# Where the low halves of the trunk weights are made: VectorE subtraction, or ScalarE negation and an accumulating DMA

## The chip, the core and the metric

The kernel runs on one core of a Trainium2 chip. The metric is device time in microseconds (us), median of the runs shown. All times are of the device alone: the host only lays the arrays out and puts the outputs together.

## What is computed

The reference is one inference step of a hybrid layer for 1,056 tokens of width 1,024 (1,024 of a prompt, 32 of a decoding request that shares the weights). Cut to what matters:

```python
z = rms_norm(x, g_mix) @ w_in                     # q, k, v, conv h/B/C, two gates
a = window_attention(q, k, v) @ w_attn_out
bo = (cb * causal_conv3(cc * ch)) @ w_conv_out
x = x + (sigmoid(ga) * a + sigmoid(gb) * bo) @ w_mix_out
cq = rms_norm(x, g_cross) @ w_cq                  # 1024 x 256
x = x + softmax(cq @ mem_k / 8) @ mem_v @ w_co    # 256 x 1024
x = x + square(relu(rms_norm(x, g_mlp) @ w_up)) @ w_down
y = rms_norm(x, g_final)
```

All of it is in fp32. The four matrices that the change speaks of are `w_conv_out` and `w_mix_out` (1,024 x 1,024 each), `w_cq` and `w_co`.

## The kernel before

**Products in two halves.** A product is made of three matmuls in the fp32r type. Each operand is split into a high part (the value rounded to fp32r) and a low part (what is left): `hi*hi + hi*lo + lo*hi`. `gemm` (L195 to L202) issues the three per 128 rows of the contraction: line L200 takes the weight's high half `wh` with the activation's high half, L201 `wh` with the low half of the activation, L202 the weight's low half `wl`. A weight tile is 128 x 1,024 (512 KB) and serves 24 matmuls of one chunk of tokens. The tokens are cut into three chunks of 384, 384 and 288 columns.

**The weights' way in.** `worder` lists the weights in the order of their use. `fetch_w` (from L145) loads the next one from HBM into a raw tile by SyncE's queue (L159). There are two raw tiles `wr`; from a certain item on (`third`, item 12 of the first chunk's trunk) every third weight goes to a third tile of another pool. `issue_w` (L164) makes `wh` by a ScalarE copy and `wl` by a VectorE subtraction, raw minus high (`split`, L128: L129 is the copy, L130 the subtraction). `wh` and `wl` have three buffers each. `next_w` runs this so that two or three weights stand ready ahead of the matmuls (`LOOK = 2`).

**Kept low halves.** The trunk is run once per chunk of tokens, so its weights come three times. For 8 of the 20 tiles (`kept`: the odd ones of `w_mix`, `w_cq` and `w_co`, and tiles 1 and 7 of `w_conv_out`), `wl` is written to a tile `wl_d` in HBM after it has been made (L179) and is loaded from there at the next uses (L172), so that VectorE isn't needed for it again; the raw tile is then needed for ScalarE's copy alone. For `w_cq` and `w_co` this ends before the third chunk.

**The stretch around the change.** The trunk lies between 797 and about 1,128 us of the profiled execution. Chunk 0: eight tiles of `w_conv_out`, the first of chunk 1, then eight of `w_mix`; no other product runs on TensorE beside them. Chunk 1: seven tiles of `w_conv_out`, eight of `w_mix`, with the cross attention of chunk 0 between them. Chunk 2: the same with 288 columns, with the cross attention of chunk 1 and the first tiles of `w_up` (the MLP) between them; at the end `w_co` of chunk 2. In the trunk, VectorE multiplies each result by a gate (L1068), and GpSimd adds the attention's part, which SyncE loads from `m_d` (L1064); that add (L1069) is where the operand of the next matrix comes from. For `w_mix`, GpSimd adds up squares for the norm (L276, L272).

**What sets the order.** The kernel is recorded with a scheduler that works on a modelled timeline and decides in which order each engine gets its instructions, within what the tiles' dependencies allow; instructions in `pin(...)` keep the order of the program. On the chip each engine, and each engine's DMA queue, then works strictly in that order: an instruction that waits holds up all that stand behind it on its engine.

Of the kernel before, what the change touches and what calls it, by code (L numbers as in the profile page):

```python
# [10 lines left out]
F32 = mybir.dt.float32  # L11
F32R = mybir.dt.float32r
AF = mybir.ActivationFunctionType
ALU = mybir.AluOpType
# [26 lines left out]
def hybrid_step(ctx: ExitStack, tc: tile.TileContext, io):  # L41
    nc = tc.nc
    act, dve, pool_e, pe, sp = nc.scalar, nc.vector, nc.gpsimd, nc.tensor, nc.sync
# [3 lines left out]
    def nm(s):  # L47
        uid[0] += 1
        return f"{s}_{uid[0]}"
# [78 lines left out]
    def split(hi, lo, src):  # L128
        act.copy(hi, src)  # L129
        dve.tensor_sub(lo, src, hi.bitcast(F32))  # L130

    def weight(key):
# [8 lines left out]
            src = src[j]  # L141
        return src

    fetched = []
    third = {}  # L145

    def fetch_w(raw=None):
        if raw is not None:
            pass
        elif third:  # L150
            third["n"] += 1
        if raw is not None:
            pass
        elif third and third["n"] % 3 == 0:
            raw = third["pool"].tile([P, 4, 256], F32, tag="ws", name=nm("wr3")).rearrange("p q c -> p (q c)")
        else:
            raw = wp.tile([P, 1024], F32, tag="wr", bufs=2, name=nm("wr"))
        src = weight(worder[wpos[0] + len(fetched)])
        load = sp.dma_start(raw.rearrange("p (i c) -> p i c", i=4) if len(src.shape) == 3 else raw, src)  # L159
        if third and third["n"] == 3 and third["pool"] is W["pool"]:  # L160
            pin(load)
        fetched.append(raw)

    def issue_w(pieces=(slice(0, 1024),)):  # L164
        if not fetched:
            fetch_w()
        raw = fetched.pop(0)
        key = worder[wpos[0]]
        hi = wp.tile([P, 1024], F32R, tag="wh", name=nm("wh"))
        lo = wp.tile([P, 1024], F32R, tag="wl", name=nm("wl"))  # L170
        if kept.get(key) is not None:
            sp.dma_start(lo.bitcast(F32), kept[key])  # L172
            act.copy(hi, raw)
        else:
            for at in pieces:
                split(hi[:, at], lo[:, at], raw[:, at])
            if key in kept:
                kept[key] = dram.tile([P, 1024], F32, name=nm("wl_d"))
                sp.dma_start(kept[key], lo.bitcast(F32))  # L179
        ready.append((worder[wpos[0]], (hi, lo)))  # L180
        wpos[0] += 1

    def next_w(key):
        while len(ready) <= LOOK and wpos[0] < len(worder) and worder[wpos[0]] is not STOP:
            issue_w()
        k, w = ready.pop(0)
        assert k == key, (k, key)
        return w
# [106 lines left out]
    def norm_x():  # L295
# [45 lines left out]
        with tc.manual_schedule(engines={mybir.EngineType.Activation, mybir.EngineType.DVE}):  # L341
            parts(0, range(1))
            issue_w((slice(0, 256), slice(256, 1024)))
            parts(0, range(1, NF))
            act.copy(ones_r, ones.to_broadcast([P, P]))
            issue_w()
            issue_w()
            squares(0)
# [115 lines left out]
    def do_K(pr, extras=()):  # L464
        def fn(w):
            kt = at_tile([P, NT], F32, "kt")
            ktt[pr] = kt
            for c, (o, n) in enumerate(CH):
                a = acc_tile([P, n])
                gemm(a, w, xg[c])  # L470
                dve.tensor_mul(kt[:, o : o + n], a, R[c])
                after(extras, c)
            sp.dma_start(io["o_k"][pr], kt[:, 896:])

        return fn
# [22 lines left out]
    def do_Q(kv, j, extras=()):  # L498
        def fn(w):
            for c, (o, n) in enumerate(CH):  # L500
                npr = min(n, NPR - o)
                if j == 0:
                    qs[kv, c] = at_tile([P, 4, npr], F32R, "QA" if c < 2 else "QB", 2 if c < 2 else 1)
                    if n > npr:
                        qs[kv, 3] = at_tile([P, 4, n - npr], F32R, "QC")
                a = acc_tile([P, n])
                gemm(a, w, xg[c])
                t = tmp(n)
                dve.scalar_tensor_tensor(t, a, 0.125, R[c], op0=ALU.mult, op1=ALU.mult)
                parts = [(qs[kv, c], slice(0, npr))]  # L510
                if n > npr:
                    parts.append((qs[kv, 3], slice(npr, n)))
                for q, s in parts:
                    for e in range(2):
                        own, other = slice(64 * e, 64 * e + 64), slice(64 - 64 * e, 128 - 64 * e)
                        h = 2 * j + e
                        act.copy(q[own, h], t[own, s])
                        dve.tensor_sub(q[other, h], t[own, s], q[own, h].bitcast(F32))
                after(extras, c)

        return fn
# [156 lines left out]
    def do_gate(to, extras=()):  # L678
        def fn(w):
            for c, (o, n) in enumerate(CH):  # L680
                a = acc_tile([P, n])
                gemm(a, w, xg[c])
                t = gate_slot(c, 0)
                dve.tensor_mul(t, a, R[c])
                act.activation(t, t, AF.Sigmoid)
                to(c, t)
                after(extras, c)

        return fn
# [18 lines left out]
    pieces = [("g", f, q) for f in PAIRS for q in range(2)]  # L708
# [42 lines left out]
    for i, h in enumerate(hosts):  # L751
# [16 lines left out]
        if h[0] == "Q":  # L768
            fn, key = do_Q(h[1], h[2], extras), qt(h[1], h[2])
        elif h[0] == "K":  # L770
            fn, key = do_K(h[1], extras), ("w_in", 8 + h[1])
        elif h[0] == "G":
            fn, key = do_gate(lambda c, t: sa.__setitem__((c, 0), t), extras), ("w_in", 34)
        else:
            fn, key = do_conv(*h, extras), conv_w(h[1], h[0])
# [932 lines left out]
    at = {}  # L1708
# [314 lines left out]
```

## Time and profile before

| | |
|---|---|
| median of 2 runs | 1754.41 us (1752.73 to 1756.1) |
| span of the profiled execution | 1747.8 us |
| TensorE busy (matmul) | 1727.7 us, 99% |
| VectorE busy | 1188.1 us, 68% |
| ScalarE busy | 852.9 us, 49% |
| GpSimd busy | 586.2 us, 34% |
| low halves made on VectorE (L130, `wl`, all weights) | 214 x 1,285 ns |
| DMA bytes moved | 346.60 MB |

The profile shows one execution. For that execution the profiler gives the span, from the first to the last instruction; the time of a run, measured without the profiler, is 4.9 to 8.3 us more than this span, 6.6 us at the median. In the rows, "busy" is the time in which an engine executes; an idle time is given with what ended it. SPq and POOLq are the queues from which SyncE and GpSimd issue DMAs. A line number is that of the kernel before.

### The profile page before, as it was taken

The numbers are of one execution on the slowest core, as the hardware profiler recorded it, in microseconds if no ns is written. First come the engines' busy times: TensorE is split into PE (matmuls) and PEld (weight loads), VectorE is DVE, ScalarE is ACT, GpSimd is POOL, SyncE is SP. The second block draws the span as 40 slices with busy tenths as digits, with TensorE's granted clock in tenths as the row PEclk, the third lists the DMA queues.
The fourth block names the chain that finished last, engine by engine and source line by source line (L and its number), as shares of the span: only waits on it lengthen the run. The fifth ranks groups of instructions, "written<-read, shape, count | busy, mean of one in ns | idle before, by whom it ended". The sixth has DMA issues, their size and how long they took to land. (4 is left out here: it accounts for less than half of the span.)

```text
span 1747.8 us, 32606 instructions
## 1 busy us (share of the span) xinstructions
PE 1727.7 (99%) x12262; PEld 1712.4 (98%) x12262; DVE 1188.1 (68%) x2276; ACT 852.9 (49%) x1660; POOL 586.2 (34%) x667
## 2 busy tenths in 40 slices
PE   9999999999999999999999999999999999999998
PEld 8999999999999999999999999999999999999998
DVE  7776777768666646555677888787666686545675
ACT  8653534535335324434556666765444463332444
POOL 0026366443553544432224232005555410000121
PEclk9999999999999999999999999999999999999999
DMA  4333344333436888867766667775666695555554
GB/s 185 104 126 128 114 134 153 115 139 127 160 132 204 296 292 280 291 203 238 264 213 198 221 227 241 235 258 191 217 222 219 219 330 185 188 193 169 192 170 160
DMA packets 179854, 346.60 MB, mean 198 GB/s; under 512 B 18657, under 2 KB 101249, under 8 KB 179569
## 3 DMA queue, kind: packets, MB, share of 16 engines
q1 hardware_dynamic: 163504, 290.07, 50.0%
q0 software_dynamic: 15568, 53.68, 8.8%
q8 instruction: 96, 1.57, 0.4%
q10 hardware_dynamic: 624, 0.77, 0.1%
q14 instruction: 62, 0.50, 0.1%
HBM read 250.73 MB, written 93.14 MB: 197 GB/s over the span
## 5 line engine op out<-in xcount | busy, mean ns | idle before, releaser
L129 ACT CAST wh<-wr 128x1024 fp32r<-128x1024 f32 (+1 forms) x214 | 223.8, 1046 | 366.6 <-PE acc L1810 121.4
L130 DVE TENSOR_TENSOR wl<-wr,wh 128x1024 fp32r<-128x1024 f32 (+1 forms) x214 | 275.0, 1285 | 106.2 <-ACT wh L129 105.4
L200 PE MATMUL acc<-X,wh 128*128 128x384 f32 (+1 forms) x864 | 281.5, 326 | 0.0
L201 PE MATMUL acc<-X,wh 128*128 128x384 f32 (+1 forms) x864 | 278.8, 323 | 0.1
L202 PE MATMUL acc<-X,wl 128*128 128x384 f32 (+1 forms) x864 | 277.8, 322 | 0.0
L276 POOL TENSOR_TENSOR xacc<-xacc,ct 128x384 f32<-128x384 f32 (+1 forms) x56 | 75.6, 1354 | 379.9 <-ACT ct L274 378.1
L201 PEld LDWEIGHTS acc<-X,wh 128*128 128x128 f32 x864 | 162.7, 188 | 1.7 <-DVE X L280 0.7
L200 PEld LDWEIGHTS acc<-X,wh 128*128 128x128 f32 x864 | 162.4, 188 | 0.8
L202 PEld LDWEIGHTS acc<-X,wl 128*128 128x128 f32 x864 | 162.4, 188 | 0.1
L200 PE MATMUL acc<-Y,wh 128*128 128x384 f32 (+1 forms) x432 | 139.9, 326 | 3.2 <-DVE ct L1068 2.9
L202 PE MATMUL acc<-Y,wl 128*128 128x384 f32 (+1 forms) x432 | 140.0, 325 | 2.7 <-DMA wl<-wl_d 2.7
L201 PE MATMUL acc<-Y,wh 128*128 128x384 f32 (+1 forms) x432 | 139.7, 324 | 0.0
L129 ACT CAST PTh<-pt 128x512 fp32r<-128x512 f32 (+3 forms) x94 | 45.8, 516 | 112.8 <-PE pt L598 111.4
L1809 PE MATMUL acc<-n,wh 128*128 128x264 f32 x352 | 100.2, 285 | 0.0
L1810 PE MATMUL acc<-n,wh 128*128 128x264 f32 x352 | 100.1, 284 | 0.0
L1811 PE MATMUL acc<-n,wl 128*128 128x264 f32 x352 | 99.9, 284 | 0.0
L735 POOL TENSOR_TENSOR ws<-ws 128x256 f32<-128x256 f32 x100 | 89.5, 895 | 5.6
L735 POOL TENSOR_TENSOR xacc<-xacc 128x256 f32<-128x256 f32 x100 | 86.8, 868 | 5.7 <-DMA xacc<-in_w_in 0.4
L200 PEld LDWEIGHTS acc<-Y,wh 128*128 128x128 f32 x432 | 81.4, 189 | 4.4 <-DVE ct L1068 3.8
L202 PEld LDWEIGHTS acc<-Y,wl 128*128 128x128 f32 x432 | 81.5, 189 | 3.0 <-DMA wl<-wl_d 3.0
L201 PEld LDWEIGHTS acc<-Y,wh 128*128 128x128 f32 x432 | 81.6, 189 | 0.0
L584 ACT ACTIVATE S<-S,nmx 128x257 f32<-128x257 f32 (+1 forms) x132 | 64.2, 488 | 18.9 <-DVE nmx L579 17.6
(432 smaller groups left out, 5554.9 us busy)
## 6 DMA issues: line engine op xcount, KB each, us to landing
wr<-in_w_up SPq DMA_DIRECT2D x53, 512.0 KB, 4.5
wr<-in_w_in SPq DMA_DIRECT2D x52, 512.0 KB, 3.6
wr<-wsum_d SPq DMA_DIRECT2D x40, 512.0 KB, 3.5
wr<-in_w_conv_out SPq DMA_DIRECT2D x24, 512.0 KB, 3.9
wr<-in_w_mix SPq DMA_DIRECT2D x24, 512.0 KB, 5.2
wr<-in_w_down SPq DMA_DIRECT2D x24, 512.0 KB, 3.6
n_d<-Z SPq DMA_DIRECT2D x32, 264.0 KB, 4.2
xacc<-in_w_down POOLq DMA_DIRECT2D x16, 512.0 KB, 4.5
```

The costliest lines, as they stand in the source:

```text
L129: act.copy(hi, src)
L130: dve.tensor_sub(lo, src, hi.bitcast(F32))
L200: pe.matmul(out, wh[:, a], hi, start=(k == 0), stop=False)
L201: pe.matmul(out, wh[:, a], lo, start=False, stop=False)
L202: pe.matmul(out, wl[:, a], hi, start=False, stop=(k == len(acts) - 1))
L276: pool_e.tensor_tensor(acc, acc, sq, op=ALU.add)
L584: act.activation(stl[:, h, : nk + 1], stl[:, h, : nk + 1], AF.Exp, scale=-1.0, bias=nmx[:, h : h + 1], accum_out=den[:, h : h + 1],)
L735: pin(pool_e.tensor_tensor(t[:, to], t[:, x], t[:, y], op=ALU.add))
L1809: pe.matmul(a, wh[:, s], hi, start=(t == 0 and k == 0), stop=False, skip_group_check=True)
L1810: pe.matmul(a, wh[:, s], lo, start=False, stop=False, skip_group_check=True)
L1811: pe.matmul(a, wl[:, s], hi, start=False, stop=(t == 1 and k == 7), skip_group_check=True)
```

## The change

```diff
+    BY_DMA = ("w_conv_out", "w_mix", "w_cq", "w_co")
...
         else:
-            for at in pieces:
-                split(hi[:, at], lo[:, at], raw[:, at])
+            if key[0] in BY_DMA:
+                act.copy(hi, raw)
+                act.mul(lo, hi.bitcast(F32), -1.0)
+                pool_e.dma_start(lo, raw, accum_op=ALU.add)
+            else:
+                for at in pieces:
+                    split(hi[:, at], lo[:, at], raw[:, at])
             if key in kept:
                 kept[key] = dram.tile([P, 1024], F32, name=nm("wl_d"))
                 sp.dma_start(kept[key], lo.bitcast(F32))
```

For a weight of the four matrices whose low half isn't loaded from `wl_d`, ScalarE makes the high half as before, and then writes its negative into `wl`. A DMA from GpSimd's queue then adds the raw weight to what stands in `wl`: minus high plus raw. VectorE has no part in it. The low halves of all other weights (`w_in`, `w_up`, `w_down`, the sums) are made as before. There are 46 such weights: 20 of `w_conv_out`, 16 of `w_mix`, 5 of `w_cq`, 5 of `w_co`. In the program, VectorE's instructions go from 2,061 rows to 2,015, ScalarE's from 1,321 to 1,367, GpSimd's from 509 to 555.

Behind the whole diff the line numbers grow by six (L1069 of before is L1075 after, L276 is L282, L810 is L816), between its two parts by one (L159 is L160), and those of `split` stay. After the change, L177 is ScalarE's copy, L178 the negation, L179 the accumulating DMA.

On GpSimd, at the beginning of chunk 0's trunk, before: the additions `ct` (L1069) of one `w_conv_out` tile after the other.

```order
L735 TENSOR_TENSOR ws_7775<-ws_7775 128x256 x4
L739 DMA usum_d<-ws_7775 128x2x256 x2
L1069 TENSOR_TENSOR ct_9363<-ct_9363,ct_9336 128x384
L1069 TENSOR_TENSOR ct_9415<-ct_9415,ct_9388 128x384
L1069 TENSOR_TENSOR ct_9467<-ct_9467,ct_9440 128x384
L1069 TENSOR_TENSOR ct_9519<-ct_9519,ct_9492 128x384
```

The same place after; `wl` is a low half, `wr` a raw tile, and the numbers are those of the buffers' use.

```order
L179 DMA wl_9256<-wr_9191 128x1024
L179 DMA wl_9278<-wr_9260 128x1024
L1075 TENSOR_TENSOR ct_9366<-ct_9366,ct_9339 128x384
L179 DMA wl_9335<-wr_9284 128x1024
L1075 TENSOR_TENSOR ct_9419<-ct_9419,ct_9392 128x384
L179 DMA wl_9388<-wr_9385 128x1024
L1075 TENSOR_TENSOR ct_9472<-ct_9472,ct_9445 128x384
L179 DMA wl_9441<-wr_9438 128x1024
```

Each addition is now followed by a DMA; the DMA of weight number n stands behind the addition that belongs to weight n-2.

On GpSimd at the change from chunk 0's `w_mix` to chunk 1's `w_conv_out`, after. Before, the additions L1069 of chunk 1's tiles stood behind each other here.

```order
L179 DMA wl_10147<-wr_10144 128x1024
L282 TENSOR_TENSOR xacc_9327<-xacc_9327,ct_10184 128x384
L1075 TENSOR_TENSOR ct_10226<-ct_10226,ct_10199 128x384
L1075 TENSOR_TENSOR ct_10267<-ct_10267,ct_10240 128x384
L179 DMA wl_10195<-wr_10192 128x1024
L179 DMA wl_10236<-wr_1800_10233 128x1024
```

Here two additions stand ahead of one DMA: the one of the weight next in use (`wl_10195`, tile 3 of `w_conv_out`) is behind the addition that belongs to tile 2.

On ScalarE in chunk 0's trunk, before and then after: the copy of the same two weights.

```order
L129 CAST wh_9436<-wr_9434 128x1024
L129 CAST M_9418<-ct_9415 128x384
L810 CAST Y_1600_9422<-ct_9378 128x384
L810 CAST Y_1602_9426<-ct_9380 128x384
L129 CAST wh_9488<-wr_9486 128x1024
```

```order
L177 CAST wh_9440<-wr_9438 128x1024
L178 ACTIVATE wl_9441<-wh_9440 128x1024
L129 CAST M_9475<-ct_9472 128x384
L816 CAST Y_1614_9479<-ct_9434 128x384
L816 CAST Y_1616_9483<-ct_9436 128x384
L177 CAST wh_9493<-wr_9491 128x1024
L178 ACTIVATE wl_9494<-wh_9493 128x1024
```

The negation L178 follows the copy at once; nothing stands between the two.

## The prediction

> **What bounds the kernel now.** I read the page first, then the waits of TensorE, then busy time by stretch, then the timeline of one raw weight buffer. The page's first lines:
>
> ```profile
> span 1747.8 us, 32606 instructions
> PE 1727.7 (99%) x12262; PEld 1712.4 (98%) x12262; DVE 1188.1 (68%) x2276; ACT 852.9 (49%) x1660; POOL 586.2 (34%) x667
> ```
>
> TensorE is the bound: 1727.7 of 1747.8 us, so 20 us is all that could be won by ending waits. VectorE, which the change relieves, is at 68%. Now the trunk alone, in four stretches: chunk 0 (two raw buffers), the `w_conv_out` part of chunk 1, its `w_mix` part, and chunk 2 (columns: from:to, length, busy time of PE, PEld, DVE, ACT and POOL, granted clock, DMA share, GB/s).
>
> ```profile
> 797.00:868.00 71.00, 71.00 (x409) 70.97 (x409) 44.54 (x68) 34.05 (x58) 17.96 (x12) 1.00 0.81 264
> 868.00:909.00 41.00, 38.32 (x219) 38.01 (x218) 29.80 (x49) 24.43 (x43) 12.37 (x9) 0.96 0.64 223
> 909.00:958.00 49.00, 49.00 (x295) 48.86 (x293) 37.67 (x60) 28.91 (x59) 20.20 (x17) 1.00 0.60 195
> 958.00:1128.00 170.00, 165.73 (x1249) 163.05 (x1248) 135.96 (x270) 114.98 (x246) 41.07 (x46) 1.00 0.68 225
> ```
>
> TensorE idles for 0 + 2.7 + 0 + 4.3 = 7 us in all of it. This bounds the gain: an empty VectorE could give back 7 us, 0.4%. The question is what the new way does to the lead with which weights are ready. The longest single wait of TensorE here is already one for a low half that comes by DMA:
>
> ```profile
> PE acc L202 <- DMA wl<-wl_d: 2.7, 1, 2.7
> ```
>
> The lead is set by the raw buffers. This is one turn of one of the two, in chunk 0, put together from the timelines of VectorE, SyncE's queue, ScalarE and VectorE again (start us, length), and behind it TensorE's rows as a new weight begins.
>
> ```profile
> 812.62 1.22 DVE L130 TENSOR_TENSOR wl<-wr,wh 128x1024 fp32r<-128x1024 f32 x1
> ...
> 815.15 0.38 SPq L159 DMA_DIRECT2D wr<-in_w_conv_out  x1
> ...
> 820.54 1.05 ACT L129 CAST wh<-wr 128x1024 fp32r<-128x1024 f32 x1
> ...
> 821.72 1.22 DVE L130 TENSOR_TENSOR wl<-wr,wh 128x1024 fp32r<-128x1024 f32 x1
> ```
>
> ```profile
> 817.96 0.34 PE L200 MATMUL acc<-Y,wh 128*128 128x384 f32 x1
> ...
> 822.15 0.34 PE L200 MATMUL acc<-Y,wh 128*128 128x384 f32 x1
> ```
>
> The subtraction that ends at 813.84 frees the raw tile; the load is issued at 815.15, ScalarE copies at 820.54, and the next subtraction from the same tile ends at 822.94. One turn is 9.10 us, and with two tiles a weight becomes ready every 4.55 us. TensorE uses one up in 822.15 - 817.96 = 4.19 us. So supply is already slower than use in chunk 0 and lives on its lead: the weight that is ready at 813.84 is used from 817.96 on, its low half by the third matmul, a lead of about 4.5 us. Whatever is added to a turn comes out as a stall.
>
> **The change part by part.** *VectorE:* 46 subtractions go. In chunk 0 they cost
>
> ```profile
> L130 DVE TENSOR_TENSOR wl<-wr,wh 128x1024 fp32r<-128x1024 f32 x15 | 18.3, 1219 | 5.3 <-ACT wh L129 5.3
> L129 ACT CAST wh<-wr 128x1024 fp32r<-128x1024 f32 x15 | 15.8, 1052 | 13.7 <-DMA wr<-in_w_conv_out 7.2 <-DMA wr<-in_w_mix 5.4 <-PE acc L202 1.1
> ```
>
> 46 x 1.22 = 56 us of VectorE, beside a busy TensorE: worth 0 to 7 us (above); I take 0.
>
> *ScalarE:* 46 negations, 1.05 us each by the copy of the same shape, 48 us. ScalarE is busy 34 of 71 us in chunk 0, so there is room; but each lies between the copy and the DMA, in the turn of the raw tile: +1.05.
>
> *GpSimd:* 46 DMA issues. The rows of its other 512 KB DMAs show about 0.55 us each:
>
> ```profile
> L730 POOL DMA_DIRECT2D xacc<-in_w_down x16 | 8.8, 551 | 50.4 <-DMA wsum_d<-xacc 49.3 <-issue 1.1
> L1069 POOL TENSOR_TENSOR ct<-ct,ct 128x384 f32<-128x384 f32 x8 | 12.3, 1533 | 60.2 <-DMA wr<-in_w_conv_out 33.0 <-DMA ct<-m_d 15.9 <-DVE ct L1068 8.7
> ```
>
> 25 us in all, and 18 of 71 us are busy. The queue matters more: GpSimd is in order, and DMA n stands behind the addition L1069 of weight n-2, which comes after TensorE's last matmul of that weight, a gate multiplication on VectorE and 1.53 us of its own. And behind an issue that waits for ScalarE stand the next additions, for which ScalarE's split of the next operand waits. SyncE's queue too: the raw load that waits for the accumulating DMA holds back the loads of `m_d` behind it. Where two additions stand ahead (the second order extract) the DMA waits for the tile just before the one it serves.
>
> *The accumulating DMA* isn't in the trace. Its time D from issue to landing decides everything, since only then are `wl` usable and the raw tile free. The nearest rows (KB each, median us to landing; then, for `wl_d`, shortest, median and longest; `Z<-ct` is the only DMA of GpSimd from SBUF to SBUF):
>
> ```profile
> xacc<-in_w_down POOLq DMA_DIRECT2D x16, 512.0 KB, 4.5
> xacc<-in_w_in POOLq DMA_DIRECT2D x14, 256.0 KB, 3.3
> wl_d<-wl SPq DMA_DIRECT2D x8, 512.0 KB, 3.4
> Z<-ct POOLq DMA_DIRECT2D x6, 72.0 KB, 5.3
> ```
> ```profile
> DMA to landing us min/median/max: 2.9/4.5/7.1
> ```
>
> A plain 512 KB from GpSimd's queue takes 4.5 us; 256 KB less saves 1.2, so 512 KB cost 2.4 beside a fixed part. An addition must read two operands: 4.5 if the second read is free, 6.9 if it costs all of 2.4. I take the middle, D = 5.7; a 72 KB DMA at 5.3 in a crowded part of the trunk says that less is unlikely. The ends: 2.9, the fastest 512 KB of the trace, and 9.0, twice the 4.5.
>
> The Trainium skill, "DMA: Bandwidth & Descriptors", section "Anatomy of one DMA", gives a DMA from GpSimd 2.0 us plus its bytes at 436 GB/s, an estimate of 3.2 us for a plain 512 KB; the 4.5 us above disagrees. By 3.2 the sum below would add 37 us and not 70. The skill's "Collectives: The Full Stack", section "The bandwidth ceiling", says that an adding DMA moves at half the rate of a copy because it needs two source reads; no trace here shows it, and with the first page's figures it would make 4.4 us and add about 52.
>
> *The sum, stretch by stretch.* A turn of a raw tile becomes 9.10 - 1.22 + 1.05 + D = 8.93 + D = 14.6 us.
>
> Chunk 0, two tiles: 14.6 / 2 = 7.3 us per weight against 4.19, a loss of 3.1. Of 17 weights the first two are loaded long before; 15 x 3.1 = 46.6, less 4.5 of lead: **42 us**. GpSimd's order is hidden here: through it a weight comes every two uses plus D, (4.19 + 2.2 + 5.7) / 2 = 6.0 us (2.2, an estimate: the addition's 1.53 above and a VectorE instruction of half that size), less than 7.3.
>
> Chunk 1, `w_conv_out` and `w_cq`: seven such weights with three raw tiles, 14.6 / 3 = 4.9 against 4.19: 7 x 0.7 = 5, and 3 for the DMA behind two additions (a whole D plus 2.2 is 8 at most): **8 us**.
>
> Chunk 1, `w_mix`: every other weight is kept and frees its raw tile at the copy, after 9.10 - 1.22 = 7.9 us. Two weights need (14.6 + 7.9) / 3 = 7.5 us, TensorE 8.4: **0**.
>
> Chunk 2, 288 columns: 4.19 x 288 / 384 = 3.1 us per weight. Of eight tiles of `w_conv_out` six go by DMA: (6 x 14.6 + 2 x 7.9) / 24 = 4.3, a loss of 1.2 x 8 = 10. In the rest, `w_up` and kept tiles lie between; for the eight others that go by DMA I add 5, an estimate: **15 us**.
>
> The clock: after the one stall of 2.7 us the profile grants half the clock for a while (same columns as above):
>
> ```profile
> 870.00:872.00 2.00, 0.78 (x4) 0.78 (x5) 0.26 (x2) 0.00 (x0) 0.00 (x0) 0.94 0.87 301
> 872.00:874.00 2.00, 2.00 (x8) 2.00 (x7) 2.00 (x3) 1.51 (x4) 0.34 (x1) 0.50 0.30 104
> 874.00:876.00 2.00, 2.00 (x10) 2.00 (x9) 1.86 (x4) 0.76 (x2) 0.98 (x1) 0.70 0.66 227
> ```
>
> That is 1 + 0.6 = 1.6 us of lost work each time. In chunk 0 the raw tiles hide it (two uses take 8.4 of a turn of 14.6); elsewhere three such: **5 us**.
>
> Sum: 42 + 8 + 0 + 15 + 5 = 70. On the profiled execution's span, 1747.8 + 70 = 1818; the median lies 6.6 us above the span, so **1824**.
>
> **The rivals.** *A cheap transfer.* D = 2.9, as the fastest row. Chunk 0: (11.8 / 2 - 4.19) x 15 - 4.5 = 21; then 3 for the order on GpSimd; chunk 2: (6 x 11.8 + 15.8) / 24 = 3.6, 4 + 3; the clock 2: +33, 1787. For it: source and destination are both SBUF. Against it: the 5.3 us of `Z<-ct`.
>
> *A dear transfer.* D = 9: (17.9 / 2 - 4.19) x 15 - 4.5 = 67; 7 x 1.8 + 3 = 15; 8 x 2 + 10 = 26; the clock 10: +118, 1872 and more. It decides where both reads and the write share the DMA engines, which are at 0.81 in chunk 0, or where GpSimd is held up while it issues. For the second, an addition of GpSimd that takes 0.74 us at the median has taken 1.74 beside VectorE's work; against it, the issues hardly vary (min/median/max in ns):
>
> ```profile
> L735 POOL TENSOR_TENSOR xacc<-xacc x100: 720/742/1744, 140.9 to 760.3; 128x256 f32<-128x256 f32 x100
> ...
> L1307 POOL DMA_DIRECT2D Z<-ct x8: 535/535/552, 1062.7 to 1072.7; - x8
> ```
>
> The Trainium skill, "SBUF — State Buffer", section "SBUF: two separate sides", has this rule: GpSimd cannot write its DMA descriptors while VectorE holds the port pair that they share. By that rule, the even 535 ns disagree.
>
> *Not slower.* The scheduler knows of the DMA and moves independent matmuls (the next chunk's `w_conv_out`, `w_up`, the cross attention) into the gaps, while VectorE's 56 us shorten the splits between matrices. Then TensorE stays busy: between 7 us less and 35 us more than now, about 1750. It decides if a weight's lead can be lengthened by D + 1.05 - 1.22 = 5.5 us, or if D is under about 3. For it: in chunk 1's `w_mix` the sum has no loss at all. Against it: in chunk 0, which holds 42 of the 70 us, no other product is at hand, and two raw tiles are all there are.
>
> **How the numbers follow.** Forecast, D from about 4 to 7.5: 0.66. Dear: 0.16. Cheap: 0.10. Not slower: 0.08. The range goes from the cheap end, 1787, to 1880, a little above the dear end's sum, since more than 9 us is possible; what is left out is most of "not slower" and the far end of "dear". Two per cent is 35 us, about what a measurement can tell from no change: slower by that begins at 1789.5. The forecast and the dear case are slower; the cheap one lies on the line, half of it within: slower 0.66 + 0.16 + 0.05 = 0.87, same 0.05 + 0.06 = 0.11, faster 0.02.
>
> **What would show it.** Right: the accumulating DMA lands 4.5 to 7 us after its issue; in 797 to 870 us TensorE waits for `wl` in L202, at every other weight for 5 to 6 us; `wr` loads are 14 to 15 us apart on one tile; the clock drops several times; VectorE's busy time falls by about 56 us and nobody gains; the `w_mix` part of chunk 1 shows no new wait; behind chunk 2 all is as before. Wrong: D under 3.5 or over 8; a new wait on GpSimd's L1075 or on SyncE's loads of `m_d` that is longer than that for `wl`; TensorE's waits in chunk 0 under 20 us in all.

## The result, and the profile after

The changed kernel takes 1857.69 us (median of two runs, 1855.79 to 1859.6) against 1754.41: a ratio of 1.0604, 95% interval 1.0531 to 1.0677. It is 103 us slower; 70 were forecast. The page of its profiled execution begins:

```profile
span 1857.8 us, 32698 instructions
PE 1763.0 (95%) x12262; PEld 1735.4 (93%) x12262; DVE 1139.0 (61%) x2230; ACT 896.4 (48%) x1706; POOL 613.7 (33%) x713
```

Against the page of before, the span is 110 us longer. TensorE idles for 1857.8 - 1763.0 = 95 us instead of 20, 75 more. The other 35 us are TensorE's own busy time, with the same 12,262 matmuls: the granted clock fell to 0.83, 0.92 and 0.93 in three of the four stretches below. VectorE lost 49 us of work and nobody gained from it.

The trunk by the same four stretches as in the prediction (columns: from:to, length, busy time of PE, PEld, DVE, ACT and POOL, granted clock, DMA share, GB/s):

```profile
794.00:913.00 119.00, 86.77 (x386) 81.02 (x385) 30.74 (x54) 48.94 (x75) 25.86 (x28) 0.83 0.85 221
913.00:976.00 63.00, 49.94 (x266) 47.94 (x266) 21.83 (x46) 34.56 (x59) 15.75 (x17) 0.92 0.90 244
976.00:1026.00 50.00, 48.61 (x288) 47.72 (x287) 26.86 (x51) 33.60 (x59) 23.68 (x24) 1.00 0.79 218
1026.00:1237.00 211.00, 174.66 (x1242) 168.10 (x1241) 116.72 (x255) 128.68 (x261) 50.55 (x64) 0.93 0.78 227
```

Only the third stretch, chunk 1's `w_mix`, is nearly as it was. In the others TensorE idles for 32, 13 and 36 us, where it idled 0, 2.7 and 4.3. The DMA share, 0.64 to 0.81 in those stretches before, is now 0.78 to 0.90. TensorE's waits, over the whole run (us in total, times, longest):

```profile
PE acc L208 <- DMA wl<-wr: 39.1, 22, 5.2
PE acc L206 <- ACT wh L177: 16.7, 10, 5.3
PE acc L886 <- ACT wh L129: 7.0, 1, 7.0
```

L208 waits for the accumulating DMA itself. L206 waits for ScalarE's copy of a weight that came late, since its raw tile was not free. SyncE's queue shows that directly, in 793 to 976 us:

```profile
SPq L160 <- DMA wl<-wr: 56.4, 17, 9.4
SPq L185 <- DMA wl<-wr: 22.8, 7, 5.6
```

Seventeen loads (L160) stood there until an accumulating DMA gave the raw tile back. Before, in 793 to 913 us, such a load waited for VectorE's subtraction, and for half as long:

```profile
SPq L159 <- DVE wl L130: 27.0, 9, 6.0
SPq L179 <- DVE wl L130: 12.4, 6, 4.5
```

The second line of each pair is the store of a kept low half to `wl_d`: it too waits for the accumulating DMA now, in the same queue, and holds back the raw loads behind it. No run takes this part away by itself. One such turn, put together from the timelines of SyncE's queue, ScalarE, GpSimd and SyncE's queue again:

```profile
816.17 0.33 SPq L160 DMA_DIRECT2D wr<-in_w_conv_out  x1
...
820.87 1.04 ACT L177 CAST wh<-wr 128x1024 fp32r<-128x1024 f32 x1
821.95 1.06 ACT L178 ACTIVATE wl<-wh 128x1024 fp32r<-128x1024 f32 x1
...
824.81 0.87 POOL L179 DMA_DIRECT2D wl<-wr  x1
...
831.63 0.33 SPq L160 DMA_DIRECT2D wr<-in_w_conv_out  x1
```

From load to load on this tile it is 15.5 us; 14.6 were forecast, and it was 9.1. Of the 15.5, 1.8 us lie between the end of the negation (823.01) and the issue (824.81): an addition L1075, 823.86 to 824.85, stood ahead in GpSimd's queue. The accumulating DMA in the groups, in the table of issues (KB each, median us to landing) and by its own rows:

```profile
L179 POOL DMA_DIRECT2D wl<-wr x46 | 40.2, 880 | 142.9 <-PE acc L888 50.5
...
wl<-wr POOLq DMA_DIRECT2D x46, 512.0 KB, 6.2
```
```profile
DMA to landing us min/median/max: 4.5/6.2/9.0
```

D is 6.2 us (5.7 taken), an issue 0.88 us (0.55 taken).

To see where the delay arises I compare when TensorE first uses each weight's high half with the time of the same weight in the kernel before. The growth of this difference over a stretch is that stretch's delay. The table below is made so, from the timelines; the kernel after comes out as 48 us in chunk 0, 17 in chunk 1's `w_conv_out` and `w_cq`, 2 in its `w_mix`, 43 in chunk 2. Behind that it stays between 107.6 and 108.8 us, up to the last weight compared: nothing is lost or regained after the trunk.

### The profile page after: what moved, and what is told of

It reads as the page before. It is cut to its first block, busy times and chain, and to the rows that moved or that the text cites. A ratio compares the mean times of both kernels' runs of the same rounds, so it can differ in the third digit from the quotient of the medians.

```text
span 1857.8 us, 32698 instructions
## 1 busy us (share of the span) xinstructions
PE 1763.0 (95%) x12262; PEld 1735.4 (93%) x12262; DVE 1139.0 (61%) x2230; ACT 896.4 (48%) x1706; POOL 613.7 (33%) x713
## 3 DMA queue, kind: packets, MB, share of 16 engines
q0 software_dynamic: 22192, 77.80, 15.6%
## 5 line engine op out<-in xcount | busy, mean ns | idle before, releaser
L129 ACT CAST wh<-wr 128x1024 fp32r<-128x1024 f32 (+1 forms) x168 | 175.4, 1045 | 344.0 <-PE acc L1816 124.6
L206 PE MATMUL acc<-X,wh 128*128 128x384 f32 (+1 forms) x864 | 281.4, 326 | 0.0
L130 DVE TENSOR_TENSOR wl<-wr,wh 128x1024 fp32r<-128x1024 f32 (+1 forms) x168 | 214.8, 1279 | 103.8 <-ACT wh L129 103.2
L208 PE MATMUL acc<-X,wl 128*128 128x384 f32 (+1 forms) x864 | 277.8, 321 | 0.0
L282 POOL TENSOR_TENSOR xacc<-xacc,ct 128x384 f32<-128x384 f32 (+1 forms) x56 | 69.8, 1249 | 348.7 <-ACT ct L280 347.4
L208 PE MATMUL acc<-Y,wl 128*128 128x384 f32 (+1 forms) x432 | 147.1, 342 | 27.7 <-DMA wl<-wr 24.6
L206 PEld LDWEIGHTS acc<-X,wh 128*128 128x128 f32 x864 | 162.4, 188 | 0.8
L208 PEld LDWEIGHTS acc<-X,wl 128*128 128x128 f32 x864 | 162.4, 188 | 0.1
L206 PE MATMUL acc<-Y,wh 128*128 128x384 f32 (+1 forms) x432 | 145.7, 339 | 11.6 <-ACT wh L177 7.0
L207 PE MATMUL acc<-Y,wh 128*128 128x384 f32 (+1 forms) x432 | 145.0, 336 | 0.0
L208 PEld LDWEIGHTS acc<-Y,wl 128*128 128x128 f32 x432 | 86.1, 200 | 32.1 <-DMA wl<-wr 28.8
L206 PEld LDWEIGHTS acc<-Y,wh 128*128 128x128 f32 x432 | 86.0, 199 | 14.5 <-ACT wh L177 8.6
L179 POOL DMA_DIRECT2D wl<-wr x46 | 40.2, 880 | 142.9 <-PE acc L888 50.5
L207 PEld LDWEIGHTS acc<-Y,wh 128*128 128x128 f32 x432 | 85.8, 199 | 0.0
```

The source lines that it names most:

```text
L206: pe.matmul(out, wh[:, a], hi, start=(k == 0), stop=False)
L207: pe.matmul(out, wh[:, a], lo, start=False, stop=False)
L208: pe.matmul(out, wl[:, a], hi, start=False, stop=(k == len(acts) - 1))
L282: pool_e.tensor_tensor(acc, acc, sq, op=ALU.add)
```

## The experiments

The theory after this result: a turn of a raw tile is longer by the landing of the DMA, and with two raw tiles that sets chunk 0. The rivals: GpSimd's order, ScalarE's extra pass, the price of adding, and the DMA engines as a bound of their own. Delays in us by stretch, from one profiled execution each; ratios are to the kernel before on the same chip, with their 95% interval:

| run | chunk 0 | chunk 1 conv, cq | chunk 1 mix | chunk 2 | ratio |
|---|---|---|---|---|---|
| after | 48 | 17 | 2 | 43 | 1.0604 [1.0531, 1.0677] |
| VectorE adds the raw weight | 14 | -5 | 1 | 11 | 1.0097 [1.0069, 1.0125] |
| DMA copies, does not add | 35 | 9 | 0 | 21 | 1.0364 [1.0333, 1.0396] |
| additions on VectorE | 44 | 14 | 2 | 38 | 1.0588 [1.0558, 1.0617] |
| DMA adds from HBM | 30 | 8 | 1 | 33 | 1.0426 [1.0391, 1.0461] |
| from HBM, additions on VectorE | 40 | 7 | 3 | 37 | 1.0473 [1.0440, 1.0505] |
| third raw tile, additions on VectorE | 32 | 15 | 2 | 34 | 1.0464 [1.0443, 1.0485] |
| the same, DMA copies | 21 | 10 | 0 | 16 | 1.0243 [1.0214, 1.0272] |
| the same, every second weight | 25 | 0 | 5 | 25 | 1.0304 [1.0271, 1.0336] |
| chunk 1's `w_mix` alone | 0 | -2 | 0 | 4 | 0.9988 [0.9978, 0.9997] |
| chunk 2 alone | 0 | -3 | 0 | 30 | 1.0159 [1.0138, 1.0179] |
| before, with the third raw tile | 1 | -4 | 0 | 1 | 1.0000 [0.9990, 1.0010] |

The -2 to -5 in the second column are no gain of the change: the profile of the kernel before has its one stall of 2.7 us there, and the last row, a kernel without the change, has -4 as well.

### ScalarE's part, the transfer, and the addition

The negation stays, and VectorE does the adding:

```diff
-                pool_e.dma_start(lo, raw, accum_op=ALU.add)
+                dve.tensor_add(lo, raw, lo.bitcast(F32))
```

> ScalarE still writes the negated high half, but VectorE adds the raw weight to it; no DMA. It prices ScalarE's part alone. My theory (a raw tile is held longer, TensorE runs out of weights): the turn of a raw tile is 9.10 + 1.05 = 10.15 us, 5.1 us per weight against 4.19, so chunk 0 loses 15 x 0.9 - 4.5 = 9 us and the rest nothing: about 1763 us. If only the DMA and GpSimd's queue matter: 1754 us, no change. If ScalarE's 48 us were the cost: well over 1780.

Measured: 1.0097, 17 us, where 9 were expected. So the two passes on ScalarE, one behind the other in each turn, cost a sixth of the 103 us. Chunk 0 loses 14 where 9 were expected, and chunk 2 loses 11, for which nothing had been expected.

The DMA stays but only copies:

```diff
-                pool_e.dma_start(lo, raw, accum_op=ALU.add)
+                pool_e.dma_start(lo.bitcast(F32), raw)
```

> The DMA from GpSimd's queue copies the raw weight instead of adding it (so the low half is wrong: the subtraction of the high half is left out); all waits, queues and holds stay. It prices the adding by itself. My theory, that the second operand's read costs time: the DMA lands in about 4.5 us at the median instead of 6.2, and at some 16 us of the kernel's time per us the kernel takes about 1830. If adding is free: 6.2 us again and 1858. If the adding were the whole trouble: under 1790.

Measured: 1.0364, some 64 us. From VectorE's addition to a copying DMA it is 47 us, from copying to adding another 42. The landing time fell by 1.2 us and not by the 1.7 expected, yet the time fell by those 42 us and not by the 28 expected: at 16 us of the kernel per us of landing, the landing time alone does not account for it. By this run's rows on that line, min/median/max, a copy's issue takes 0.57 us and it lands in 5.0:

```profile
L179 POOL DMA_DIRECT2D wl<-wr x46: 528/568/594, 791.8 to 1185.1; - x46
...
DMA to landing us min/median/max: 2.9/5.0/7.1
```

The larger difference is in the time for which the 16 DMA engines are held. GpSimd's queue in the pages of before, after and this run (packets, MB, share of 16 engines' span):

```profile
q0 software_dynamic: 15568, 53.68, 8.8%
```
```profile
q0 software_dynamic: 22192, 77.80, 15.6%
```
```profile
q0 software_dynamic: 22192, 77.80, 12.0%
```

8.8% of 1747.8 us is 154 us, 15.6% of 1857.8 is 290, 12.0% of this run's span, 1809.2, is 217. So 46 adding DMAs hold all engines for 136 us, 3.0 each, and 46 copies for 63 us, 1.4 each. The same bytes take twice the engines' time when they are added.

The adding DMA also converts, since its target is of the fp32r type. To tell adding from converting:

```diff
-                pool_e.dma_start(lo, raw, accum_op=ALU.add)
+                pool_e.dma_start(lo.bitcast(F32), raw, accum_op=ALU.add)
```

> The kernel after the change, with one difference: the adding DMA writes the low half as fp32 words and not as the fp32r type, so that it adds and does not convert. In the kernel after, a DMA held the 16 engines for 3.0 us and its issue took 0.87 us; the one that only copied, between fp32 words, 1.4 and 0.57. Theory that the addition (its second read) makes the difference: nothing changes, issue 0.87 us, 6.2 us to landing, 3.0 us of the engines, ratio 1.060. Rival, that the conversion of the type makes it: 0.57, 5.0 and 1.4 us, ratio 1.036.

Measured: 1.0615 [1.0592, 1.0639]. It is the addition: 6.1 us to landing, 0.87 us an issue, and the queue's share is again 15.6%, of a span of 1852.6.

```profile
wl<-wr POOLq DMA_DIRECT2D x46, 512.0 KB, 6.1
```

### GpSimd's order

All additions of the trunk go to VectorE, so that no DMA stands behind one:

```diff
-            (dve if f == NF - 1 else pool_e).tensor_tensor(t, t, t1, op=ALU.add)
+            dve.tensor_tensor(t, t, t1, op=ALU.add)
```

> The additions of the attention's part in the trunk go from GpSimd to VectorE, so that no accumulating DMA stands behind them in GpSimd's queue. My theory (the turn of two raw tiles limits chunk 0, GpSimd's order is hidden behind it): 0 to 10 us less, 1848 to 1858. Rival (GpSimd's order makes the stalls): chunk 0 and the w_conv_out parts come back, under 1810.

Measured: 1.0588, inside the interval of the kernel after. GpSimd's order is not what the time goes to while the raw tiles are the limit; it makes 4 us of chunk 0's 48 at most.

### The raw tile, freed at once

The DMA adds the weight from HBM, so that the raw tile is free after ScalarE's copy:

```diff
-                pool_e.dma_start(lo, raw, accum_op=ALU.add)
+                pool_e.dma_start(lo, weight(key), accum_op=ALU.add)
```

> The accumulating DMA reads the raw weight from HBM instead of from the raw tile, so the raw tile is free after ScalarE's copy; time of the DMA, queue and waits for the low half stay. My theory: the raw tile's turn falls to 7.9 us (3.9 per weight) and no longer limits; next comes GpSimd's order, (4.19 + 2.2 + 6.2) / 2 = 6.3 us per weight, so chunk 0 loses 15 x 2.1 - 4.5 = 27 us instead of 47, and chunks 1 and 2 lose half: about 1810. Rival (GpSimd's order alone): unchanged, 1850 to 1860. Rival (DMA traffic): the extra reads from HBM make it slower, over 1860.

Measured: 1.0426, 74 us, where 56 were expected; some 30 are won, 18 of them in chunk 0 by the table. Chunk 0 came out near the 27 expected, with 30; chunk 2 kept 33 of its 43. The raw tile's turn did cost what was won, and then something else holds. The same with the additions on VectorE (both edits above):

> Both at once: the accumulating DMA reads from HBM, and the additions of the trunk are on VectorE, so neither the raw tile nor GpSimd's additions hold a weight up. My theory: what is left is the three buffers of the low half, (2.2 + 0.9 + 6.2 + 4.19) / 3 = 4.5 us per weight against 4.19, 5 us in chunk 0, and some stalls with a slow clock in chunk 2: 1770 to 1790. Rival (DMA traffic, or the time of the DMA itself): still over 1830.

Measured: 1.0473. This is a clear miss, 40 us above the upper end (1830.35 us), where the rival of DMA traffic or DMA time had put it, and no better than without the second edit. So nothing here shows that GpSimd's order, from which the 27 us had been worked out, holds the first of the two runs. The window from the trunk's start to the end of chunk 1's `w_conv_out`, before, and then with the raw weight from HBM (second last column: DMA share):

```profile
793.00:913.00 120.00, 117.32 (x674) 116.97 (x673) 81.18 (x128) 63.43 (x113) 31.02 (x21) 0.99 0.74 246
```
```profile
793.00:947.00 154.00, 125.45 (x654) 118.96 (x653) 52.62 (x100) 84.61 (x134) 42.14 (x45) 0.92 0.98 269
```

Before, the DMA engines work 0.74 x 120 = 89 us here. 25 adding DMAs at 3.0 us bring 75 more: 164 us, against 117 us of TensorE. The run with HBM shows 0.98 x 154 = 151, somewhat less than that sum, and its engines are busy nearly throughout. This points to a second bound behind the raw tiles, one that a better order of instructions would not move. With the additions on VectorE, their operand `ct` from `m_d` is what comes late: VectorE waited for it in 793 to 905 us

```profile
DVE ct L1075 <- DMA ct<-m_d: 25.3, 6, 8.8
```

and these 192 KB loads land after 6.6 us at the median, 3.3 before. Whether that is all that keeps this run from gaining was not settled.

### A third raw tile

The third tile serves from the trunk's first weight on, and the additions are on VectorE:

```diff
-        + [(12, lambda: third.update(n=0, pool=W["pool"]))] + ...
+        + [(0, lambda: third.update(n=0, pool=W["pool"]))] + ...
```

> The third raw tile comes in at the first item of chunk 0's trunk instead of the thirteenth, and the trunk's additions are on VectorE. My theory: the turn of 15.1 us is shared by three tiles, 5.0 us per weight against 4.19, so chunk 0 loses 15 x 0.85 - 4.5 = 8 us instead of 47; the rest as before: about 1818. Rival (the number of raw tiles does not matter; the DMA's time or the traffic does): 1845 or more.

Measured: 1.0464, or 1828.81 us, some 21 better than with the additions alone. Chunk 0 lost 32 us and not 8. Two things stand against a larger gain. The first load into the third tile was issued only at 819 us, and it brought the sixth weight of the trunk. And the engines are full again:

```profile
793.00:958.00 165.00, 132.26 (x668) 126.74 (x667) 61.40 (x117) 86.69 (x137) 29.01 (x32) 0.91 0.95 252
```

0.95 x 165 = 157 us of engine time, near the sum above. To tell the engines from the mere landing time, the same with the copying DMA, and with every second weight by DMA:

```diff
+            turn[0] += key[0] in BY_DMA
-            if key[0] in BY_DMA:
+            if key[0] in BY_DMA and turn[0] % 2:
```

> Third raw tile from the start of the trunk and all additions on VectorE, as in the run before with these two edits, but the DMA copies the raw weight and does not add it: the subtraction of the high half is left out, so the low half is wrong by that. A copying DMA held the 16 DMA engines for 1.4 us of their time each, an adding one for 2.9. Theory that the DMA engines are the next bound once a third raw tile is there: to the end of chunk 1's w_conv_out they need 83 us for the other queues and 25 x 1.4 = 35, 118 us against TensorE's 112, so that the delay up to there is 6 to 15 us in place of the 46 measured with the adding DMA; chunk 2 delays by some 21, as with the copying DMA and two raw tiles: about 30 to 36 us above before, ratio 1.018 to 1.021. Rival, that only the time from issue to landing counts (6.5 us to 5.0): with three tiles 0.5 us per weight, 12 of the 46 us go, and the ratio stays at about 1.03.

> The same two edits, adding DMA, but only every second of the 46 weights goes by it (23); the others are split by VectorE as before. Theory of the DMA engines as the next bound: 83 + 12 x 2.9 = 118 us of their time up to the end of chunk 1's w_conv_out, so 6 to 15 us of delay there, and in chunk 2 about half of the 34 us: 25 us above before, ratio 1.014. If instead the delay comes from each single adding DMA that lands late, half of the 80 us stay: ratio 1.023.

Measured: 1.0243 and 1.0304, both outside what either theory gave. With copies the delay up to the end of chunk 1's `w_conv_out` falls from 46 to 31 us (6 to 15 by the engines' theory, 34 by the rival), and in chunk 2 from 34 to 16. With half the weights 53 us remain, more than 25 or 40. Over the whole window the engines are no longer full:

```profile
793.00:943.00 150.00, 129.24 (x668) 124.24 (x667) 60.56 (x118) 86.54 (x137) 21.09 (x32) 0.92 0.83 278
```
```profile
793.00:934.00 141.00, 122.40 (x654) 118.50 (x653) 70.75 (x123) 71.56 (x117) 17.53 (x19) 0.94 0.85 247
```

But the window mixes two stretches. Cut at chunk 0 alone, from HBM, with a third tile, the same with copies, and the same with every second weight:

```profile
793.40:894.10 100.70, 78.10 (x387) 72.64 (x386) 28.66 (x54) 49.98 (x75) 27.08 (x29) 0.90 0.98 268
```
```profile
796.00:898.50 102.50, 79.30 (x387) 75.27 (x387) 33.99 (x60) 48.78 (x73) 18.00 (x20) 0.90 0.99 263
```
```profile
795.40:886.90 91.50, 77.03 (x388) 74.15 (x387) 33.24 (x60) 49.26 (x74) 12.72 (x20) 0.91 0.85 285
```
```profile
793.50:889.00 95.50, 79.34 (x410) 76.32 (x409) 44.42 (x71) 43.59 (x69) 12.02 (x13) 0.93 0.92 266
```

The engines' time is 99 and 101 us in the first two, where the stretch took 71 us before. As far as these transfers have to lie in chunk 0, that alone is a delay of 28 and 30 us, of the 30 and 32 measured. (The 27 us worked out from GpSimd's order for the first of them may then have come near by chance.) With copies it is 78 us, 7 of 21, and with half the weights 88 us, 17 of 25.

So the engines' time is a floor that the runs with adding DMAs and freer raw tiles reach (0.98, 0.99 in chunk 0), and where it is lower the chain of each single weight still delays. TensorE's waits for a low half by DMA, with half the weights, over the whole run:

```profile
PE acc L209 <- DMA wl<-wr: 19.0, 10, 5.6
```

Ten waits of TensorE for the 23 DMAs that are left. How these 53 us divide into late raw tiles, the order on the queues and the clock stays open.

### Where it costs nothing, and where more than thought

Only four tiles of chunk 1's `w_mix`, and only chunk 2 (`times` counts the uses of a weight so far):

```diff
-    BY_DMA = ("w_conv_out", "w_mix", "w_cq", "w_co")
+    BY_DMA = ("w_mix",)
...
+            times[key] = times.get(key, 0) + 1
-            if key[0] in BY_DMA:
+            if key[0] in BY_DMA and times[key] == 2:
```
```diff
+        times[key] = times.get(key, 0) + 1
...
-            if key[0] in BY_DMA:
+            if key[0] in BY_DMA and times[key] == 3:
```

> Only the four w_mix tiles of chunk 1 that aren't kept go by accumulating DMA, 4 of 46. My theory: every other weight there frees its raw tile early, the lead covers the DMA, and it costs nothing: 1751 to 1757 us. Rival (each such DMA costs its share, 103 / 46 = 2.2 us): about 1763.

> Only chunk 2's weights go by accumulating DMA, 14 of 46. The changed kernel lost 43 us there where the sum had 15. If the loss belongs to this stretch itself (fewer columns per weight, other queues' work between, a slow clock): about +40, 1795 us. If it came down from the earlier chunks (a lead that was used up): about +15, 1770.

Measured: 0.9988 for the first, as expected: where every other weight is a kept one, a DMA of 6 us is covered. The second gives 1.0159, 28 us, between what the two theories gave, 40 and 15: most of chunk 2's loss arises there, and the rest only with the chunks before. The longest single wait there is not at a tile of the trunk. In the kernel after, on TensorE, SyncE's queue, ScalarE and TensorE again:

```profile
1161.55 0.40 PE L208 MATMUL acc<-Y,wl 128*128 128x288 f32 x1 [1.03 <-DMA wl<-wr]
...
1166.52 1.17 SPq L160 DMA_DIRECT2D wr<-in_w_up  x1
...
1173.08 2.00 ACT L129 CAST wh<-wr 128x1024 fp32r<-128x1024 f32 x2 [5.42 <-DMA wr<-in_w_up]
...
1174.18 0.59 PE L886 MATMUL acc<-Z,wh 128*128 128x264 f32 x1 [6.95 <-ACT wh L129]
```

Two tiles of `w_cq` by DMA stand ahead of this tile of `w_up`, which takes the raw tile of the first. That one's low half had landed at 1161.5, when TensorE could use it (first row). The load followed at 1166.5, behind other DMAs of SyncE's queue, and TensorE stood for 6.95 us. In the run with chunk 2 alone the same wait is 5.4 us.

Last, the third raw tile in the kernel before, without the change:

> The kernel before, with the third raw tile from the trunk's first item instead of its thirteenth. Supply in chunk 0 was 4.55 us per weight against a use of 4.19 and lived on its lead, without a wait of TensorE. If that is right nothing is to be won: ratio 1.000, within 0.002. If the change's loss came from a supply that had been short already, the ratio falls below 0.997.

Measured: 1.0000 [0.9990, 1.0010]. The old supply had not been short, and no version here beats the kernel before by more than the 0.1% of the `w_mix` run.

## Why the prediction was right, and by how much it was short

The sign and the main mechanism, the longer turn of the raw tiles, held, and 1857.69 lies in 1787 to 1880. The forecast itself was 34 us too low. That the range held is in part luck: with the measured D = 6.2 the prediction's own sum gives 46 + 9 + 0 + 15 + 5 = 75, thus 1829; what covers the measured time is the upper end, taken for a DMA of 9 us, which it isn't.

- *VectorE's 56 us are worth nothing:* right. VectorE's busy time fell by 49 us, and TensorE only waited more.
- *The negation adds 1.05 us to a turn:* right in size (1.06). Alone, with VectorE adding, it cost 17 us in place of the 9 worked out for that run.
- *An issue costs 0.55 us:* mis-sized. An adding DMA's takes 0.88; a copy's takes 0.57.
- *D = 5.7, a copy's 4.5 and half a second read, 1.2:* the surcharge came out exactly, 6.2 - 5.0, though it was only the middle between two bounds. The base was 0.5 short: a copy lands in 5.0 here.
- *Chunk 0, 42 us:* 48. With D = 6.2 the prediction's own formula gives (15.1 / 2 - 4.19) x 15 - 4.5 = 46. This step holds, and the longer raw-tile turn is shown by SyncE's waits, 56 us for 27, and by the 18 us that come back in chunk 0 when the DMA adds from HBM.
- *GpSimd's order is hidden:* right, 1.0588 without it, and 4 us less in chunk 0.
- *Chunk 1's `w_conv_out` and `w_cq`, 8 us:* mis-sized, 17. The formula gives 9 with D = 6.2. The DMA share there is 0.90, and in the run with a third tile and copying DMAs the stretch still costs 10; what made the other 8 was not singled out.
- *Chunk 1's `w_mix`, 0:* right, 2, and none when done alone.
- *Chunk 2, 15 us:* this step failed, 43, and 28 when done alone. The 5 us "for the eight others" was a guess. It left out that `w_up` and the other weights use the same raw tiles, so that a late tile of the trunk passes its delay on to them; the wait of 7.0 us shows this once. Of the 36 us that TensorE idles in this chunk, 17.5 are waits for a low half by DMA. The negation alone makes 11 of the 43, a copying DMA 21. How the rest divides is open.
- *The clock, 5 us outside chunk 0:* mis-sized. TensorE's busy time rose by 35 us in all, in chunk 0 by 87 - 71 = 16 and in chunk 2 by 175 - 166 = 9, as cut by the windows; outside chunk 0 that leaves 19. Chunk 0's share lies inside its 48, as the prediction had it: the raw tiles set that time.
- *The median lies 6.6 us above the span:* not so after the change, 1857.69 against a span of 1857.8. The two come from different executions. So the 110 us by spans are 103 by medians, and the sum itself, 70, was 40 short.

What the prediction left out of its sum is the time of the DMA engines. The dear rival named it, at D = 9. D stayed at 6.2, but the engines' 3.0 us per DMA add up to some 150 to 160 us in a stretch of 120. This is the likely reason why freeing the raw tile, or adding a third, gave back only 16 to 18 of chunk 0's 48 us: the engines are at 0.98 and 0.99 there. It is not shown apart from the time to landing, since the copying DMA shortens both.

Of the rivals, the cheap one falls: D is 6.2, and even a copy's 5.0 costs 64 us. "Not slower" falls: even with a third raw tile the change costs 81 us. Of the signs named beforehand, one had the wrong shape. TensorE does not wait 5 to 6 us at every other weight in chunk 0. It waits 1.8 us on average, nine times for a low half and nine times for a copy, and the rest of the loss is slow matmuls.

## What to carry to other kernels

A buffer that a DMA reads is held until that DMA lands; moving a 1.2 us instruction of an engine with time to spare into a 6 us DMA lengthens each turn of that buffer. So divide the turn by the number of buffers and compare it with the use before anything else. Then sum the time for which the DMA engines are held, stretch by stretch, since adding took twice that of copying here; more buffers do not move that sum. Off-loading an engine that is not the bound wins nothing, but where every other item frees its buffer early such a DMA can be free.

## What the runs showed of the hardware that was not expected

*Adding in a DMA.* The engines are held 3.0 us for 512 KB added and 1.4 us for 512 KB copied, while the time to landing grows by only 1.2 us, and GpSimd's issue from 0.57 to 0.87 us. Converting to fp32r costs nothing beside it. The Trainium skill, "Collectives: The Full Stack", section "The bandwidth ceiling: the fold count and why AG ≠ RS ≠ AR", says of ReduceScatter's adding transfers that they run at half the rate of AllGather's copies, because an add needs two source reads. The engines' time here agrees with that, a factor of 2.1; the time to landing, a factor of 1.2, does not.

*The clock.* Some short waits cost more than their length. TensorE and the granted clock (columns as above) around one wait in chunk 0 of the kernel after (a DMA share over 1 is possible in a short window, since a transfer counts whole where it starts):

```profile
825.48 0.45 PE L208 MATMUL acc<-Y,wl 128*128 128x384 f32 x1 [2.00 <-DMA wl<-wr]
...
828.31 0.52 PE L207 MATMUL acc<-Y,wh 128*128 128x384 f32 x1
...
830.62 0.34 PE L207 MATMUL acc<-Y,wh 128*128 128x384 f32 x1
```
```profile
826.00:828.00 2.00, 2.00 (x10) 2.00 (x9) 0.92 (x2) 0.22 (x1) 0.00 (x0) 0.63 0.93 178
828.00:830.00 2.00, 2.00 (x8) 2.00 (x8) 0.00 (x0) 0.00 (x0) 0.00 (x0) 0.52 1.10 240
```

The wait of 2.00 us ends at 825.48. From about 826.5 the matmuls take 0.52 us instead of 0.34, for 3.4 us. The shorter wait before it in this chunk, 0.87 us, was not followed by this, and one of 1.88 us, at 833.02, was:

```profile
818.70 0.44 PE L206 MATMUL acc<-Y,wh 128*128 128x384 f32 x1 [0.87 <-ACT wh L177]
...
822.45 0.34 PE L206 MATMUL acc<-Y,wh 128*128 128x384 f32 x1
...
833.02 0.44 PE L206 MATMUL acc<-Y,wh 128*128 128x384 f32 x1 [1.88 <-ACT wh L177]
...
834.20 0.52 PE L207 MATMUL acc<-Y,wh 128*128 128x384 f32 x1
```

Where between the two the limit lies was not measured. The Trainium skill, "TensorE: Matmul & The Clock Gate", section "Part 1: The HAM clock gate (the \"warmup\" mystery)", gives half the clock after an idle window of about 3.4 us; the wait of 2.00 us was shorter and had the same effect.
